# The level products of gated linear attention as 128-key matmuls, and as column tiles of 32 keys

## The chip, the core and the metric

The kernel runs on one core of a Trainium2 chip. The metric is the device time of one execution in microseconds, as the median of several runs: 2526.48 us before the change (three runs, 2525.47 to 2529.76). One more execution was taken with the hardware profiler; all rows come from it.

The engines appear in the profile as PE (matmuls) and PEld (the weight loads ahead of them), DVE (VectorE), ACT (ScalarE), POOL (GpSimd) and SP (the engine that issues most DMAs).

## The reference, cut to what matters

The model is one layer of a decoder trunk on a sequence of 2048 tokens with 1024 channels, in f32: a token mixer with three groups of heads (4 retention heads, 8 HGRN2 heads, 4 GLA heads), then a gated MLP with a short convolution. The change touches only the HGRN2 and GLA heads. Their recurrence, with a decay per key channel, is

```python
cum = jnp.cumsum(gn, axis=2)
rel = jnp.where(causal, cum[:, :, :, None, :] - cum[:, :, None, :, :], -jnp.inf)
attn = jnp.einsum('bhid,bhjd,bhijd->bhij', qn, kn, jnp.exp(rel))
o = jnp.einsum('bhij,bhje->bhie', attn, vn) + jnp.einsum('bhid,bhde->bhie', qn * jnp.exp(cum), s)
```

So query i meets key j with the product of all decays between them, channel by channel, and only for j up to i.

## The kernel before, in words

**Blocks and units.** The sequence is cut into 4 blocks of 512 tokens (TB), each into 4 chunks of 128 tokens. In a block the mixer works through seven units in the order h, g, h, h, h, r, r (ORDER, L35): four HGRN2 units of two heads (`unit_h`, L715), one GLA unit of four heads (`unit_g`, L754) and two retention units (`unit_r`, L799). Each unit first makes its projections: large matmuls on operands split into a high and a low part, three matmuls for one product (`split3`, L236). These are the bulk of PE's work. After the four blocks follow the out projection and the MLP.

**Levels.** A chunk's causal triangle is built by halving (`gated`, L618). For a level s of 1, 2, 4, ..., 64 (LEVELS, L604) tokens are grouped in blocks of 2s: the second half of each block are queries, the first half keys. `q` and `kq` already hold the decay up to the level's block borders, so one plain product gives the attention of all such pairs; then `q` and `kq` are multiplied by the decays of the next level (L648 and L650 on DVE) and the next level follows.

**The level product.** For each chunk L642 multiplies all 128 keys of the chunk with the 64 odd-half queries of each of two heads: 128 columns, written to 128 PSUM rows. Of each column only the s rows of the query's own block are wanted. A GLA unit has two parts of 64 channel rows each, whose products are issued in turn. A g unit so has 8 products for a level and an h unit 4. There are 16 h units and 4 g units, with 7 levels each: 112 h levels and 28 g levels.

**Taking out what is wanted.** For s up to 16 DVE copies all 512 columns from PSUM into the attention tile `at` (128 x 1024), under a mask `m_all` (L659, `copy_predicated`). For s of 32 and 64 ACT copies the wanted blocks (L656). `at` is set to zero before by POOL (L627). The attention tiles meet the values in `attn_out` (L600); the dot products of a token with itself are made apart (`dots`, L632).

**What sets the order.** PE's instructions stand in the order in which the program writes them. A planner (`Clock`, L55) interleaves the units' chains with the projections: each matmul moves a counter of microseconds on by an assumed price (`adv`, with M512 = 0.227 for a 512-column matmul and MF = 0.224 for an f32 product), and a chain's next step is due a gap later. After a level the gap is 3.2 us for h and 4.2 us for g (LEVEL_GAP, L51); projections fill it. A unit's chain begins when the one before has written its outputs' last step (`yield None`). The other engines' order is set by the scheduler from dependencies and priorities; what stands on an engine's queue waits in order, SP's and POOL's included. `lev` has two PSUM banks, `q` (`new_qbd`, L531, set to zero by POOL in L535) three buffers, `at` shares eight buffers of 4 KB. The table of rotary angles (`rope`, L802) has one buffer and is loaded once per block (L803) for the retention units. The masks are loaded by one DMA at the start (L1075); everything else of the first block is issued behind it.

**Other lines that the prediction uses.** L761 and L762 are a product with a weight of only 32 columns (`alow`, the low-rank gate of the GLA heads), which is written to PSUM rows 0 to 31. L664 are the transposes that follow a unit's last level. L597 are the products of queries with the state. L615 makes the decays of the levels. L820 is the first use of the rotary table.

Of the kernel before, what the change touches and what calls it, by code (L numbers as in the profile page):

```python
# [9 lines left out]
F32 = mybir.dt.float32  # L10
F32R = mybir.dt.float32r
I32 = mybir.dt.int32
U32 = mybir.dt.uint32
# [4 lines left out]
P = 128  # L18
# [28 lines left out]
HOT = 600  # L47
CHAIN = 400

M512, M256, MF = 0.227, 0.12, 0.224  # L50
LEVEL_GAP = (3.2, 4.2)  # L51
POST_GAP = 12.0

# [1 line left out]
class Clock:  # L55
# [15 lines left out]
    def adv(self, us):  # L71
        self.t += us
        while self.due and self.due[0][0] <= self.t:
            self._next()
# [26 lines left out]
def trunk(ctx, tc, xT, vecs, cvec, cst, rope, msk, wada, win, walow, wgla, wout, wup, wdown, out):  # L101
    nc = tc.nc
# [9 lines left out]
    pu = mix.enter_context(tc.tile_pool(name="unit", bufs=2))  # L112
    p1 = mix.enter_context(tc.tile_pool(name="const1", bufs=1))
    pp = ctx.enter_context(tc.tile_pool(name="ps", bufs=1, space=PSUM))
    clock = Clock()
    adv = clock.adv
# [4 lines left out]
    def lev_ps(name):  # L121
        return pp.tile([P, 512], F32, tag="lev", name=name, bufs=2)
# [3 lines left out]
    def late_ps(name):  # L126
        return pp.tile([P, 512], F32, tag="late", name=name, bufs=2)
# [10 lines left out]
    V, S, G, T = nc.vector, nc.scalar, nc.gpsimd, nc.tensor  # L138
# [1 line left out]
    vec = pc.tile([P, 117], F32, tag="vec", name="vec")  # L140
    nc.sync.dma_start(vec[:], vecs[:, 0:117])
    c_all = pc.tile([P, NC_], F32, tag="cst", name="c_all")
    m_all = p1.tile([P, 320], U32, tag="msk", name="m_all")
    ident = c_all[:, C_ID:C_ID + P]
    causal = c_all[:, C_CAUS:C_CAUS + P]
    ones = c_all[:, C_ONE:C_ONE + 1]
# [95 lines left out]
    h = [None] * KD  # L242
# [346 lines left out]
    def attn_out(name, b, attn, v, qn, Sst):  # L589


        ps = late_ps("o" + name)
        for c in range(NCH):
            oc = ps[:, c * P:(c + 1) * P]
            inter = not (b == 0 and c == 0)
            if inter:
                T.matmul(oc, qn[:, c * P:(c + 1) * P], Sst[:, (b * NCH + c) % NS, :], start=True, stop=False)  # L597
            for hh in range(2):
                at, col = attn[hh]
                T.matmul(oc[:, hh * 64:hh * 64 + 64], at[:, (c * 2 + col) * P:(c * 2 + col + 1) * P],  # L600
                         v[:, c, hh * 64:hh * 64 + 64], start=not inter, stop=hh == 1 or not inter)
        return ps
# [15 lines left out]
    def gated(name, b, ui, pos, kq, q, decay, subs, qk, sel):  # L618

        Sst = states[ui]  # L620
        tree, cur = decay
        two = len(subs) > 1
        parts = [slice(0, 64), slice(64, P)] if two else [slice(0, P)]
        attns = []
        for i, _ in enumerate(subs):
            at = pa.tile([P, 8 * P], F32, tag="a4k", name=f"at{name}_{i}")
            G.memset(at[:], 0.0)  # L627
            attns.append(at)
        nh = 2 * len(subs)
        ps = late_ps("dt" + name)  # L630
        for c in range(NCH):
            T.matmul(ps[:, c * nh:(c + 1) * nh], qk[:, c * P:(c + 1) * P], sel, start=True, stop=True)  # L632
        dots = pu.tile([P, NCH * nh], F32, tag="dots", name="dot" + name, bufs=3)
        S.copy(dots[:], ps[:, 0:NCH * nh])
        adv(4 * MF)
        for li, s in enumerate(LEVELS):
            nb = 64 // s
            pss = [lev_ps(f"lv{name}_{s}") for _ in parts]
            for c in range(NCH):
                for ps, rs in zip(pss, parts):  # L640
                    rhs = q[rs, :, c * P:(c + 1) * P].rearrange("p h (n t s) -> p h n t s", t=2, s=s)[:, :, :, 1, :]
                    T.matmul(ps[:, c * P:(c + 1) * P].rearrange("p (h n s) -> p h n s", h=2, s=s),  # L642
                             kq[rs, c * P:(c + 1) * P], rhs, start=True, stop=True)
            with tc.high_priority(offset=CHAIN):
                ev = tree[li]
                nn = TB // (2 * s)
                qv = q[:].rearrange("p h (n t s) -> p h n t s", t=2, s=s)[:, :, :, 1, :]
                V.tensor_tensor(qv, qv, ev[:, :, 0:1].unsqueeze(1).to_broadcast([P, 2, nn, s]), op=ALU.mult)  # L648
                kv = kq[:].rearrange("p (n t s) -> p n t s", t=2, s=s)[:, :, 0, :]
                V.tensor_tensor(kv, kv, ev[:, :, 1:2].to_broadcast([P, nn, s]), op=ALU.mult)  # L650
                for ps, at in zip(pss, attns):
                    dst = at[:].rearrange("p (a n t s) -> p a n t s", a=8, t=2, s=s)[:, :, :, 1, :]
                    src = ps[:].rearrange("p (a n s) -> p a n s", a=8, s=s)
                    if s >= 32:
                        for j0 in range(0, P, 2 * s):
                            S.copy(dst[j0:j0 + s, :, j0 // (2 * s), :], src[j0:j0 + s, :, j0 // (2 * s), :])  # L656
                    else:
                        mk = m_all[:, li * 64:li * 64 + 64].rearrange("p (n s) -> p n s", s=s)
                        V.copy_predicated(dst, mk.unsqueeze(1).to_broadcast([P, 8, nb, s]), src)  # L659
            adv(4 * MF)  # L660
            yield LEVEL_GAP[two]
        ps = late_ps("kT" + name)
        for c in range(NCH):
            T.transpose(ps[:, c * P:(c + 1) * P], kq[:, c * P:(c + 1) * P], ident)  # L664
        kT = pu.tile([P, NCH, P], F32, tag="kT", name="kT" + name, bufs=1)
        with tc.high_priority(offset=CHAIN):
            S.copy(kT[:].rearrange("p c n -> p (c n)"), ps[:])
            if not two:
                r0, r1 = subs[0][0][1]
                S.copy(q[r0:r1, 0, :], q[r0:r1, 1, :])  # L670
        adv(4 * MF)
        yield 1.8
        for rows, v, sg in subs:
            ps = late_ps("u" + name)
            for c in range(NCH):
                T.matmul(ps[:, c * P:(c + 1) * P], kT[:, c, :], v[:, c, :], start=True, stop=True)
            with tc.high_priority(offset=CHAIN):
                for c in range(NCH):
                    for hh, (r0, r1) in enumerate(rows):
                        es = slice(64 * hh, 64 * hh + 64)  # L680
                        dst = Sst[r0:r1, (b * NCH + c + 1) % NS, es]
                        u = ps[r0:r1, c * P + hh * 64:c * P + hh * 64 + 64]
                        if b == 0 and c == 0:
                            V.tensor_copy(dst, u)
                        elif c < NCH - 1 or b < NB - 1:
                            V.scalar_tensor_tensor(dst, Sst[r0:r1, (b * NCH + c) % NS, es], cur[r0:r1, c:c + 1], u,
                                                   op0=ALU.mult, op1=ALU.add)
        adv(4 * len(subs) * MF)
        yield 2.2
        os = []  # L690
        for i, (rows, v, sg) in enumerate(subs):
            if i:
                yield 2.2
            o = pu.tile([P, NCH, P], F32, tag="o", name=f"o{name}_{i}")
            dd = dots[:].rearrange("p (c h) -> p c h", h=nh)[:, :, 2 * i:2 * i + 2]
            o4 = o[:].rearrange("p c (h e) -> p c h e", e=64)
            with tc.high_priority(offset=CHAIN):
                V.tensor_tensor(o4, v[:].rearrange("p c (h e) -> p c h e", e=64),
                                dd.unsqueeze(3).to_broadcast([P, NCH, 2, 64]), op=ALU.mult)
            heads = [(at, i) for at in attns] if two else [(attns[0], hh) for hh in range(2)]  # L700
            ps = attn_out(f"{name}_{i}", b, heads, v, q[:, i, :], Sst)
            adv(12 * MF)
            with tc.high_priority(offset=CHAIN):
                V.tensor_tensor(o[:].rearrange("p c e -> p (c e)"), o[:].rearrange("p c e -> p (c e)"), ps[:],
                                op=ALU.add)
                post(o, sg, f"{name}_{i}")
            os.append(o)
        yield None
        for i, o in enumerate(os):
            yield POST_GAP if i == 0 else 3.0  # L710
            transposed(b, pos + i, o, f"{name}_{i}")
            adv(4 * MF)
# [356 lines left out]
    mk = {"h": unit_h, "g": lambda b, u, pos: unit_g(b, pos), "r": unit_r}  # L1069
    PE, DVE, ACT, SP = (getattr(mybir.EngineType, n) for n in ("PE", "DVE", "Activation", "SP"))  # L1070
    ctx.enter_context(tc.manual_schedule(engines={PE}))
    with tc.manual_schedule(engines={DVE, ACT, SP}):
        W0 = startup()
        last = gla_weights()
        first = [nc.sync.dma_start(m_all[:], msk[:, 0:320]).ins, *last]  # L1075
    jobs = [job for k in range(NF // 2) for job in (("d", k), ("u", 2 * k + 1 if k < 10 else 0))]
    behind = ExitStack()
    for ins in first:
# [538 lines left out]
```

## Time and profile before

| what | value |
|---|---|
| median of three runs | 2526.48 us |
| profiled execution, its own time | 2525.46 us |
| its span in the profile, first to last instruction | 2523.6 us |
| PE busy in the span | 2481.0 us, 98% |
| DVE busy | 1945.3 us, 77% |
| ACT busy | 1135.4 us, 45% |
| POOL busy | 159.7 us, 6% |
| mean granted TensorE clock | 0.996 |

The profile lists groups of instructions as line, engine, operation, output<-inputs with the tiles' names (lvh and lvg are the level banks of h and g units, ath and atg the attention tiles, X, Z, dX and others the MLP's banks), the shape, and the count. An f32 matmul appears as two records, each with its own weight load. A matmul's duration contains the way through the array, so successive matmuls overlap in the records; the distance of their starts tells what one costs. "128\*32" in a row means 128 contraction rows and 32 weight columns; "x512" the columns that stream through.

### The profile page before, as it was taken

The numbers are of one execution on the slowest core, as the hardware profiler recorded it, in microseconds if no ns is written. First come the engines' busy times: TensorE is split into PE (matmuls) and PEld (weight loads), VectorE is DVE, ScalarE is ACT, GpSimd is POOL, SyncE is SP. The second block draws the span as 40 slices with busy tenths as digits, with TensorE's granted clock in tenths as the row PEclk, the third lists the DMA queues.
The fourth block names the chain that finished last, engine by engine and source line by source line (L and its number), as shares of the span: only waits on it lengthen the run. The fifth ranks groups of instructions, "written<-read, shape, count | busy, mean of one in ns | idle before, by whom it ended". The sixth has DMA issues, their size and how long they took to land. (4 is left out here: it accounts for less than half of the span.)

```text
span 2523.6 us, 37047 instructions
## 1 busy us (share of the span) xinstructions
PE 2481.0 (98%) x13175; PEld 2110.3 (84%) x13175; DVE 1945.3 (77%) x3566; ACT 1135.4 (45%) x1913; POOL 159.7 (6%) x271
## 2 busy tenths in 40 slices
PE   7999999999999999999999999999999999999998
PEld 5888888888889888888888888888887888888887
DVE  7788976868678676767888888886688777778666
ACT  4443434423434235333455455455445554545542
POOL 1000000000000000000010000000001010010000
PEclk9999999999999999999999999999999999999999
DMA  8455576675687846885654544487665444447663
GB/s 296 174 190 171 207 266 210 230 270 200 220 325 260 284 156 235 289 295 177 235 184 148 170 149 141 159 299 240 209 222 180 153 138 153 152 132 259 222 194 124
DMA packets 228074, 524.95 MB, mean 208 GB/s; under 512 B 24968, under 2 KB 28080, under 8 KB 227888
## 3 DMA queue, kind: packets, MB, share of 16 engines
q1 hardware_dynamic: 224688, 512.08, 59.6%
q0 software_dynamic: 3200, 10.49, 1.2%
q8 instruction: 104, 1.70, 0.3%
q14 instruction: 82, 0.67, 0.1%
HBM read 392.97 MB, written 129.50 MB: 207 GB/s over the span
## 5 line engine op out<-in xcount | busy, mean ns | idle before, releaser
L238 PE MATMUL X<-B,A 128*128 128x512 f32 x572 | 223.1, 390 | 1.7 <-ACT u L1295 1.7
L239 PE MATMUL X<-B,A 128*128 128x512 f32 x572 | 222.6, 389 | 0.0
L240 PE MATMUL X<-B,A 128*128 128x512 f32 x572 | 222.5, 389 | 0.0
L1007 DVE TENSOR_TENSOR dA<-rd,dA 128x512 fp32r<-128x512 f32 x154 | 105.9, 689 | 90.4 <-ACT dA L1006 90.2
L1006 ACT CAST dA<-rd 128x512 fp32r<-128x512 f32 x154 | 95.5, 621 | 143.8 <-PE dX L240 57.3
L239 PE MATMUL dX<-dB,dA 128*128 128x512 f32 x396 | 154.2, 389 | 1.7 <-DVE dB L1007 1.7
L238 PE MATMUL dX<-dB,dA 128*128 128x512 f32 x396 | 154.1, 389 | 1.2 <-DVE y L1475 1.2
L240 PE MATMUL dX<-dB,dA 128*128 128x512 f32 x396 | 154.1, 389 | 0.0
L1007 DVE TENSOR_TENSOR A<-s,A 128x512 fp32r<-128x512 f32 x176 | 120.5, 685 | 38.6 <-ACT A L1006 38.5
L238 PE MATMUL psvgh<-hvgh,ha 128*128 128x256 f32 x480 | 140.8, 293 | 0.0
L1006 ACT CAST A<-s 128x512 fp32r<-128x512 f32 x176 | 108.6, 618 | 69.8 <-PE Z L240 40.3
L240 PE MATMUL psvgh<-hvgh,ha 128*128 128x256 f32 x480 | 136.4, 284 | 0.0
L239 PE MATMUL psvgh<-lvgh,ha 128*128 128x256 f32 x480 | 136.3, 284 | 0.0
L238 PEld LDWEIGHTS X<-B,A 128*128 128x128 f32 x572 | 107.4, 188 | 24.8 <-ACT u L1295 2.8
L240 PEld LDWEIGHTS X<-B,A 128*128 128x128 f32 x572 | 107.4, 188 | 22.4
L239 PEld LDWEIGHTS X<-B,A 128*128 128x128 f32 x572 | 107.4, 188 | 22.2
L239 PE MATMUL Z<-B,A 128*128 128x512 f32 x308 | 120.3, 390 | 1.6 <-DVE B L1007 1.6
L642 PE MATMUL lvh<-qbh,kh 128*128 128x128 f32 x896 | 120.2, 276 | 1.5 <-DVE nw L157 1.3
L642 PEld LDWEIGHTS lvh<-qbh,kh 128*128 128x128 f32 x896 | 114.7, 190 | 8.0 <-issue 2.0
L238 PE MATMUL Z<-B,A 128*128 128x512 f32 x308 | 120.3, 391 | 0.5 <-ACT B L1006 0.5
L240 PE MATMUL Z<-B,A 128*128 128x512 f32 x308 | 119.8, 389 | 0.0
L1007 DVE TENSOR_TENSOR A<-r,A 128x512 fp32r<-128x512 f32 x132 | 90.5, 686 | 26.4 <-ACT A L1006 26.1
(470 smaller groups left out, 7008.2 us busy)
## 6 DMA issues: line engine op xcount, KB each, us to landing
gs<-yv SPq DMA_DIRECT2D x154, 256.0 KB, 2.8
rb<-gs SPq DMA_DIRECT2D x154, 256.0 KB, 4.0
r<-wup SPq DMA_DIRECT2D x143, 256.0 KB, 3.3
s<-sumsu SPq DMA_DIRECT2D x132, 256.0 KB, 3.0
wada<-wada SPq DMA_DIRECT2D x48, 512.0 KB, 4.6
rd<-sumsd SPq DMA_DIRECT2D x88, 256.0 KB, 4.0
rd<-wdown SPq DMA_DIRECT2D x66, 256.0 KB, 3.8
x<-xT SPq DMA_DIRECT2D x64, 256.0 KB, 5.3
```

Source lines behind the costliest of these rows:

```text
L238: T.matmul(ps, lhs[0], rhs[0], start=first, stop=False, skip_group_check=more)
L239: T.matmul(ps, lhs[0], rhs[1], start=False, stop=False, skip_group_check=more)
L240: T.matmul(ps, lhs[1], rhs[0], start=False, stop=last, skip_group_check=more)
L642: T.matmul(ps[:, c * P:(c + 1) * P].rearrange("p (h n s) -> p h n s", h=2, s=s), kq[rs, c * P:(c + 1) * P], rhs, start=True, stop=True)
L1006: S.copy(hi, src)
L1007: V.tensor_tensor(lo, src, hi, op=ALU.subtract)
```

## The change

A level product is cut into pieces of w = max(32, 2s) tokens. For s up to 16 a chunk gives four products: 32 keys with the 32 odd-half queries (both heads) of the same 32 tokens, and each writes to the 32 PSUM rows of its keys, that is to its own strip of 32 columns of the PE array. For s = 32 there are two products of 32 keys with 64 columns, for s = 64 one of 64 keys with 128 columns. The four chunks lie side by side in the bank: a level of s up to 16 fills 128 columns instead of 512. An h unit has 16, 8 and 4 products for the three kinds of level, a g unit 32, 16 and 8.

For s up to 16 DVE copies these 128 columns under a smaller mask into a small tile `near` (128 x 8 x 32), which POOL sets to zero once per part of a unit. After level 16 ACT spreads `near` to its place in `at` with four copies of 32 rows and 256 columns. `near` has one buffer; the second one, of g units, shares the buffer of the rotary table (tag "rope"). The copies for s of 32 and 64 stay on ACT, with the same sizes. The masks are loaded by four DMAs of 32 rows. The planner counts 0.5 us (ML) for a level instead of 4 x MF = 0.896.

```diff
-M512, M256, MF = 0.227, 0.12, 0.224
+M512, M256, MF, ML = 0.227, 0.12, 0.224, 0.5
...
-    m_all = p1.tile([P, 320], U32, tag="msk", name="m_all")
+    m_all = p1.tile([P, 5, 16], U32, tag="msk", name="m_all")
...
-        attns = []
+        attns, nears = [], []
         for i, _ in enumerate(subs):
             at = pa.tile([P, 8 * P], F32, tag="a4k", name=f"at{name}_{i}")
             G.memset(at[:], 0.0)
             attns.append(at)
+            near = pu.tile([P, 8, 32], F32, tag="rope" if i else "near", name=f"near{name}_{i}", bufs=1)
+            G.memset(near[:], 0.0)
+            nears.append(near)
...
         for li, s in enumerate(LEVELS):
-            nb = 64 // s
+            w, keys = max(32, 2 * s), min(max(32, s), 64)
+            cols = slice(0, 8 * w // 2)
             pss = [lev_ps(f"lv{name}_{s}") for _ in parts]
             for c in range(NCH):
-                for ps, rs in zip(pss, parts):
-                    rhs = q[rs, :, c * P:(c + 1) * P].rearrange("p h (n t s) -> p h n t s", t=2, s=s)[:, :, :, 1, :]
-                    T.matmul(ps[:, c * P:(c + 1) * P].rearrange("p (h n s) -> p h n s", h=2, s=s),
-                             kq[rs, c * P:(c + 1) * P], rhs, start=True, stop=True)
+                for r0 in range(0, P, w):
+                    at = c * P + r0
+                    for ps, rs in zip(pss, parts):
+                        rhs = q[rs, :, at:at + w].rearrange("p h (n t s) -> p h n t s", t=2, s=s)[:, :, :, 1, :]
+                        T.matmul(ps[r0:r0 + keys, c * w:(c + 1) * w].rearrange("p (h n s) -> p h n s", h=2, s=s),
+                                 kq[rs, at:at + keys], rhs, start=True, stop=True)
...
-                for ps, at in zip(pss, attns):
-                    dst = at[:].rearrange("p (a n t s) -> p a n t s", a=8, t=2, s=s)[:, :, :, 1, :]
-                    src = ps[:].rearrange("p (a n s) -> p a n s", a=8, s=s)
-                    if s >= 32:
-                        for j0 in range(0, P, 2 * s):
-                            S.copy(dst[j0:j0 + s, :, j0 // (2 * s), :], src[j0:j0 + s, :, j0 // (2 * s), :])
+                for ps, at, near in zip(pss, attns, nears):
+                    if s <= 16:
+                        mk = m_all[:, li, :].rearrange("p (n s) -> p n s", s=s)
+                        V.copy_predicated(near[:].rearrange("p a (n t s) -> p a n t s", t=2, s=s)[:, :, :, 1, :],
+                                          mk.unsqueeze(1).to_broadcast([P, 8, 16 // s, s]),
+                                          ps[:, cols].rearrange("p (a n s) -> p a n s", a=8, s=s))
                     else:
-                        mk = m_all[:, li * 64:li * 64 + 64].rearrange("p (n s) -> p n s", s=s)
-                        V.copy_predicated(dst, mk.unsqueeze(1).to_broadcast([P, 8, nb, s]), src)
-            adv(4 * MF)
+                        for r0 in range(0, P, w):
+                            S.copy(at[r0:r0 + s, :].rearrange("p (a n) -> p a n", a=8)[:, :, r0 + s:r0 + 2 * s],
+                                   ps[r0:r0 + s, cols].rearrange("p (a n) -> p a n", a=8))
+                    if s == 16:
+                        for r0 in range(0, P, 32):
+                            S.copy(at[r0:r0 + 32, :].rearrange("p (a n) -> p a n", a=8)[:, :, r0:r0 + 32],
+                                   near[r0:r0 + 32])
+            adv(ML)
...
-        first = [nc.sync.dma_start(m_all[:], msk[:, 0:320]).ins, *last]
+        masks = msk[:, 0:320].rearrange("p (l n) -> p l n", n=64)
+        first = [nc.sync.dma_start(m_all[32 * g:32 * g + 32], masks[32 * g:32 * g + 32, :, 16 * g:16 * g + 16]).ins
+                 for g in range(4)] + last
```

## The prediction

> **What bounds the kernel now.** I read the table by stretches first, then the waits of PE, then the groups by line and shape, then the timeline around single levels.
>
> ```profile
> 63.00:350.00 287.00, 285.70 (x1824) 253.07 (x1824) 243.90 (x534) 116.02 (x215) 12.15 (x20) 1.00 0.56 196
> 960.00:1200.00 240.00, 237.85 (x1501) 207.69 (x1500) 169.64 (x402) 96.95 (x186) 13.72 (x22) 1.00 0.72 251
> 0.00:1200.00 1200.00, 1174.60 (x7308) 1027.50 (x7309) 915.81 (x2098) 478.66 (x886) 65.03 (x108) 1.00 0.67 235
> ```
>
> Columns: stretch, its length, then busy us (and count) of PE, PEld, DVE, ACT, POOL; PEclk, DMA share, GB/s. The mixer, where the change lies, is 0 to 1200 us. From 63 us on PE leaves 1.3 us of 287 and 2.2 of 240 free, at full clock. So what PE saves there shortens the run, and what another engine saves does not, unless PE waits for it. It hardly does:
>
> ```profile
> PE og L597 <- DVE S L686: 1.8, 1, 1.8
> PE psvgg L238 <- ACT qg L770: 1.4, 1, 1.4
> ```
>
> These two are the longest waits of PE between 60 and 1200 us (columns: us in all, times, longest). Now the level products, with the least, median and longest duration in ns; then a load of 32 columns; then groups by shape (busy us, mean ns):
>
> ```profile
> L642 PEld LDWEIGHTS lvh<-qbh,kh x896: 186/192/193, 63.3 to 1169.5; 128*128 128x128 f32 x180
> L642 PE MATMUL lvh<-qbh,kh x896: 270/275/362, 63.4 to 1169.6; 128*128 128x128 f32 x180
> L642 PEld LDWEIGHTS lvg<-qbg,kg x448: 182/188/188, 104.0 to 1041.0; 64*128 64x128 f32 x150
> L642 PE MATMUL lvg<-qbg,kg x448: 270/272/378, 104.0 to 1041.1; 64*128 64x128 f32 x150
> ```
> ```profile
> L761 PEld LDWEIGHTS alg<-ha,alow x32: 106/108/112, 53.4 to 973.1; 128*32 128x32 f32 x32
> ```
> ```profile
> L659 DVE COPY_PREDICATED ath<-m_all,lvh 128x512 f32<-128x512 uint32 x80 | 76.1, 951 | 0.0
> ...
> L659 DVE COPY_PREDICATED atg<-m_all,lvg 128x512 f32<-128x512 uint32 x40 | 36.9, 950 | 3.5 <-PE lvg L642 3.5
> ...
> L632 PE MATMUL dth<-c_all,qkh 128*128 128x2 f32 x128 | 15.9, 246 | 0.0
> ```
> ```profile
> L656 ACT COPY ath<-lvh 32x256 f32<-32x256 f32 x32 | 11.6, 363 | 51.8 <-PE lvh L642 50.2 <-issue 1.2
> ```
>
> Each f32 matmul is two passes here (448 products in 16 h units, 896 records), each pass a weight load and a matmul. A level of an h unit is 8 passes, of a g unit 16 (two halves of 64 rows). The durations contain the pipeline's latency, so what a level costs PE is read as delay in the timeline (start, duration):
>
> ```profile
> 67.35 0.39 PE L239 MATMUL psaqg<-ha,haqg 128*128 128x512 f32 x1
> 67.58 0.39 PE L240 MATMUL psaqg<-ha,laqg 128*128 128x512 f32 x1
> 67.81 1.07 PE L642 MATMUL lvh<-qbh,kh 128*128 128x128 f32 x8
> 68.63 0.48 PE L238 MATMUL psaqg<-ha,haqg 128*128 128x512 f32 x1
> 68.95 0.40 PE L239 MATMUL psaqg<-ha,haqg 128*128 128x512 f32 x1
> ```
> ```profile
> 109.81 0.39 PE L240 MATMUL pshfh<-ha,lhfh 128*128 128x512 f32 x1
> 110.12 1.18 PE L642 MATMUL lvg<-qbg,kg 64*128 64x128 f32 x16
> 111.23 0.50 PE L238 MATMUL pshqh<-ha,hhqh 128*128 128x512 f32 x1
> 111.57 0.39 PE L239 MATMUL pshqh<-ha,hhqh 128*128 128x512 f32 x1
> ```
>
> Projection matmuls start 0.23 us apart (67.35, 67.58). From 67.58 to 68.95 are 1.37 us for two steps (0.46) and the level: **0.91 us for an h level**. From 109.81 to 111.57: 1.76 less 0.46, **1.30 for a g level**. All: 112 x 0.91 + 28 x 1.30 = 138 us, the most the change can touch.
>
> **The change part by part.** *One pass.* A weight load of 128 columns takes 190 ns (188 to 192), of 32 columns 108: 82 ns for 96 columns, so 27 ns for 32 and 109 for 128. That this load sets the pace shows in dth: 8 passes of only 2 columns are 15.9/16 = 0.99 us busy, less the last's 0.246, over 7 steps 0.107 each. A level pass is 0.91/8 = 0.114, stream and load side by side. So a pass of 32 keys by 32 columns is 27 ns of load beside at most 27 of stream: 0.032 us with the same 5 ns on top.
>
> *Do four column tiles run side by side?* No row shows it. The nearest: the g level does 16 passes in little more time than an h level does 8, so two row tiles do run together; its 1.30 is 8 x 0.114 = 0.91 plus 0.39 for going in and out. For column tiles the only row is the product of alow, 32 weight columns wide:
>
> ```profile
> 358.35 0.39 PE L240 MATMUL y<-oTr,lwo 128*128 128x512 f32 x1
> 358.58 0.39 PE L761 MATMUL alg<-ha,alow 128*32 128x512 f32 x1
> ...
> 360.20 0.40 PE L762 MATMUL alg<-ha,alow 128*32 128x512 f32 x1
> 360.44 0.38 PE L597 MATMUL oh<-S,qbh 128*128 128x128 f32 x2
> ```
>
> In 0.23, out 0.24: the plain step, no toll. [...]
>
> *Levels 1 to 16.* The 8 passes of a part and level become 4 chunks x 4 tiles x 2 passes = 32. Bounds: with the four tiles fully side by side each has 8 passes, 8 x 0.032 + 0.03 for the first load = 0.28; one after the other 32 x 0.032 = 1.02. Between them lies a third case: the two passes of a product follow each other on their tile, and only the next product runs beside them, 16 x 0.032 = 0.51. I take **0.45**, just below that, because the g row, the nearest, shows tiles that overlap almost fully. No toll is added, by the alow row. For g there are 64 passes on eight tiles: 0.28 + 0.39 = 0.67 at least, 1.02 + 0.39 = 1.41 at most. I take **0.80**, nearer to the lower end for the same reason.
>
> *Level 32.* Two tiles of 64 columns, 55 ns of stream: 8 x 0.06 + 0.03 = **0.51** (up to 16 x 0.06 = 0.96); g 0.51 + 0.39 = **0.90**. *Level 64.* One tile of 64 keys and 128 columns, stream as before: **0.91** and **1.30**.
>
> Sum: h unit 7 x 0.91 = 6.37 before, 5 x 0.45 + 0.51 + 0.91 = 3.67 after, -2.70 x 16 = -43.2. g unit 9.10 before, 5 x 0.80 + 0.90 + 1.30 = 6.20, -2.90 x 4 = -11.6. **PE: -54.8 us**, ends -71 and +12.
>
> *DVE.* The 120 masked copies fall from 512 elements to 128.
>
> ```profile
> L648 DVE TENSOR_TENSOR qbh<-qbh,eh 128x512 f32<-128x512 f32 x96 | 65.9, 686 | 38.8 <-PE lvh L642 38.0
> ...
> L615 DVE TENSOR_TENSOR eh<-eh 128x128 f32<-128x128 f32 x16 | 4.6, 289 | 0.3
> ```
>
> A plain product of two tiles goes from 0.69 to 0.29 us between these sizes; the masked copy takes 0.95/0.69 = 1.4 times the plain one, so 0.40 after: 120 x 0.55 = 66 us less on DVE. It is off the path: the next level's products wait for L648 and L650, which stand ahead of the copy, and PE's waits on DVE in the mixer are a few us in all. Value 0, between -5 (those waits gone) and 0.
>
> *ACT.* New: four copies of 32x256 per part at level 16, 24 parts, 96 x about 0.38 (L656's 0.363 from PSUM) = 36 us. They wait for the masked copy on DVE; behind them on ACT stand level 32's copies, weight casts and evacuations, for which PE waits. Cover: ACT is 40% busy (478.66 of 1200), and L656 already sits 50 us in front of lvh without a PE wait on the list. Value **+4**, between 0 and +36 if nothing covered them.
>
> *POOL.* 24 memsets of near (256 columns) join those of the attention tiles (L627), on an engine busy 65 of 1200 us. near has one buffer, so its memset waits until the unit before has spread it at level 16. Behind it on POOL stand the q memsets (L535), which wait for the output products (L597) of an earlier unit, and the first masked copy of the next unit waits for near itself:
>
> ```profile
> 102.98 1.09 POOL L535 MEMSET qbh<- 64x512 f32 x2 [57.93 <-PE oh L597]
> ```
>
> POOL stood still for 57.93 us in front of this one anyway, and the output products come two levels after the spread. So near's wait is over first: 0. If that cover went, the masked copies of the new unit's level 1 would be late, and with them the level banks.
>
> *SP.* near's second tile takes the place of the rope table:
>
> ```profile
> L820 DVE TENSOR_TENSOR rb0r<-ra0r,roper x8: 417/422/426, 233.6 to 1172.9; 128x256 f32<-128x256 f32 x8
> ...
> L803 SPq DMA_DIRECT2D roper<-rope x4: 328/376/509, 55.2 to 877.9; - x4
> ```
> ```profile
> L664 PE MATMUL kTg<-c_all,kg x16: 270/272/273, 147.1 to 1046.0; 128*128 128x128 f32 x16
> ```
> ```profile
> L1075 SPq DMA_DIRECT2D m_all<-msk x1: 420/420/420, 40.2 to 40.2; - x1
> ```
>
> The first rope load cannot go at 55.2 any more, but after g's level 16, which is over before g's transposes at 147; it is needed at 233.6. Moved down SP's queue it costs 0; left in its place, every load queued behind it would stand for up to 90 us. Three more mask loads are 3 x 0.42 = 1.3 us of SP at 40 us; behind them is the key projection's weight load (L225), in front of a PE that there waits for its first inputs: 0 to +1, value 0.
>
> *Order of the work.* The planner now counts 0.5 for a level instead of 0.896. The gaps that it fills with projections (3.2 and 4.2 us) stay, so between two levels stand as many projections as before, and a unit's chain only ends 7 x 0.4 = 2.8 planner's us earlier: 0.
>
> Sum: -54.8 + 4 = -50.8. The profiled execution took 2525.5 (span 2523.6 and 1.9 around it): 2474.7; the median shown is 1.0 higher: **2476 us**.
>
> **The rivals.**
> *1. The h levels pay g's toll of 0.39 too.* Levels 1 to 16 at 0.28 + 0.39 = 0.67, level 32 at 0.90, level 64 at 1.30: 5.55 per unit, -0.82 x 16 = -13; g as forecast: 2526.5 - 13 - 11.6 + 4 = 2506. For: the g rows. Against: the alow rows.
>
> *2. The four tiles share one path for weights or columns.* h unit 5 x 1.02 + 0.96 + 0.91 = 6.97, +0.60 x 16 = +9.6; g 5 x 1.41 + 1.35 + 1.30 = 9.70, +0.60 x 4 = +2.4; with ACT's 4: 2543. For: load time goes by columns (108 against 190 ns), and the sum of columns loaded is unchanged. Against: g's two row tiles load and stream together.
>
> *3. PE's sequencer does not deliver the instructions fast enough (the slower side).* Between two levels of an h unit stand 3.2 us of projections, 14 passes or 28 instructions; with the 64 of a level they are 92, in 3.65 us: 40 ns each. In g 4.2 us hold 37, with 128 of a level 165, in 5.0 us: 30 ns.
>
> ```profile
> 418.93:425.21 6.28, 6.28 (x65) 6.02 (x66) 5.35 (x9) 1.30 (x3) 0.00 (x0) 1.00 0.73 252
> ```
>
> The densest stretch of that length now has 131 in 6.28 us, 48 ns each, so 40 is shown nowhere. At x ns per instruction levels 1 to 16 of all units (80 of h, 20 of g, 4.11 and 5.50 us with their gaps now) change by 80 x (0.092x - 4.11) + 20 x (0.165x - 5.50), and level 32 gives 8 back: the sign turns at **42 ns**. At 48 it is +65, with ACT's 4 **2596**. For: 40 is asked of every level, and nowhere shown. Against: in g's level 32 instructions pass in about 1.1 us, 34 ns each, though only 32.
> *4. Small passes have a fixed price of their own*, whatever their size, and start x ns apart. [...] The rows leave x open: g's 16 passes in 0.91 us are 57 ns each, dictated by their weight loads. [...]
>
> *5. Half the gain is lost to waits on ACT and DVE*: Closer levels ask for copies and evacuations sooner, and DVE is 85% busy in the first block (243.90 of 287); against it, DVE gets 66 us less to do. 2526.5 - 25 = 2501.
>
> **How the numbers follow.** Forecast (2452 to 2500) 0.49, rival 1 0.12, rival 5 0.05: faster, 0.66. Rival 4 0.05: within 0.2% (about what a measurement of this kernel can tell from no change). Rival 2 0.12, rival 3 0.17: slower, 0.29. From -71 us with nothing lost (2455) to rival 2 with half of ACT's copies uncovered (2556) lies 0.82; rival 3 is left out. Range 2452 to 2556.
>
> **What would show it.** Right: 2944 h passes and 1472 g passes on the level line; from the projection matmul ahead of a level to the second one behind it about 0.91 us (0.46 + 0.45) in h for levels 1 to 16; masked copies of 128 elements near 0.40 us; no wait of PE on ACT's copies beyond the 1.4 us seen. Rival 1: same toll at level 64. Rival 2: about 1.0 per level. Rival 3: projection matmuls behind a level spread to more than 0.23 apart, PE idle with "issue". Wrong above all would be a level above 0.9, or PE waiting for ACT's spread or for near's memset.

## The result, and the profile after

The changed kernel takes 2489.76 us (median of four runs, 2488.3 to 2490.3), against 2527.95 us (2525.47 to 2529.76) for the kernel before, measured beside it: a ratio of 0.9849 with a 95% interval of 0.9832 to 0.9866, 38 us less. The profiled execution took 2489.37 us, its span is 2487.6, so 36.0 less than the 2523.6 of before.

All of it is won in the mixer: the last output product (L600 in both kernels) starts at 1174.2 us instead of 1210.5, 36.3 earlier. First the stretches, with the columns of the prediction's first fence; the mixer now ends at 1175.

```profile
63.00:350.00 287.00, 284.42 (x2769) 240.57 (x2769) 230.28 (x545) 131.32 (x249) 14.42 (x27) 1.00 0.61 206
960.00:1175.00 215.00, 214.81 (x2065) 184.31 (x2064) 146.34 (x380) 92.28 (x188) 10.95 (x20) 1.00 0.79 274
```

PE is as full as before (2.6 and 0.2 us free), with more and smaller instructions. So the gain is the PE time that the levels gave up, and nothing else was let in. The longest waits of PE between 60 and 1200 us are still single ones, and no row names ACT's spread or `near`'s memset:

```profile
PE lvh L648 <- DVE kh L656: 4.0, 1, 4.0
PE pshfh L239 <- DVE ha L350: 1.1, 1, 1.1
```

The groups of the three lines that the change made (L648 is the level product, L660 the masked copy, L669 the spread; least, median and longest ns):

```profile
L648 PE MATMUL lvh<-qbh,kh x2944: 189/196/323, 63.4 to 1134.1; 128*32 128x32 f32 x171, 128*32 128x64 f32 x17, 128*64 128x128 f32 x9
L648 PE MATMUL lvg<-qbg,kg x1472: 186/193/320, 102.5 to 1009.6; 64*32 64x32 f32 x160, 64*32 64x64 f32 x16, 64*64 64x128 f32 x8
...
L660 DVE COPY_PREDICATED nearh<-m_all,lvh x80: 284/296/455, 65.1 to 1126.5; 128x128 f32<-128x128 uint32 x80
...
L669 ACT COPY ath<-nearh x64: 387/405/412, 82.2 to 1128.2; 32x256 f32<-32x256 f32 x64
```

The counts are the forecast ones: 2944 and 1472 passes, 120 masked copies, 96 spread copies. The masked copy takes 0.30 us (forecast 0.40), the spread copy 0.40 (0.38).

What a level costs PE is read as in the prediction: from the start of the last projection matmul before it to that of the second one behind it, less two steps of 0.23. The timeline of the changed kernel around an h level of the first five, h's level 64, a g level, and the product of `alow` (start, duration):

```profile
79.74 0.39 PE L240 MATMUL psvgg<-hvgg,ha 128*128 128x512 f32 x1
80.06 0.46 PE L648 MATMUL lvh<-qbh,kh 128*32 128x32 f32 x32
80.45 0.50 PE L238 MATMUL psvgg<-hvgg,ha 128*128 128x512 f32 x1
80.79 0.39 PE L239 MATMUL psvgg<-lvgg,ha 128*128 128x512 f32 x1
...
87.95 0.39 PE L240 MATMUL psvgg<-hvgg,ha 128*128 128x512 f32 x1
88.27 1.09 PE L648 MATMUL lvh<-qbh,kh 128*64 128x128 f32 x8
89.29 0.50 PE L238 MATMUL psvgg<-hvgg,ha 128*128 128x512 f32 x1
89.63 0.40 PE L239 MATMUL psvgg<-lvgg,ha 128*128 128x512 f32 x1
...
107.86 0.39 PE L240 MATMUL pshfh<-ha,lhfh 128*128 128x512 f32 x1
108.17 0.76 PE L648 MATMUL lvg<-qbg,kg 64*32 64x32 f32 x64
108.86 0.50 PE L238 MATMUL pshqh<-ha,hhqh 128*128 128x512 f32 x1
109.19 0.40 PE L239 MATMUL pshqh<-ha,hhqh 128*128 128x512 f32 x1
...
349.45 0.40 PE L240 MATMUL y<-oTr,lwo 128*128 128x512 f32 x1
349.68 0.40 PE L772 MATMUL alg<-ha,alow 128*32 128x512 f32 x1
...
350.38 0.39 PE L773 MATMUL alg<-ha,alow 128*32 128x512 f32 x1
350.61 0.38 PE L597 MATMUL oh<-S,qbh 128*128 128x128 f32 x2
350.83 0.33 PE L600 MATMUL oh<-vh,ath 128*128 128x64 f32 x2
```

Look at the first level. Its 32 passes are in the records for 0.46 us; less the 0.20 of the last one, the last pass starts 0.26 after the first. Four tiles with eight passes each in 0.26 us are 33 ns a pass: the tiles run fully side by side. But the level begins 0.32 behind the projection matmul (79.74 to 80.06), where a plain level begins 0.23 behind it (67.58 to 67.81 in the kernel before), and the second projection matmul is 0.34 behind the first (80.45 to 80.79) instead of 0.23. That is the toll which the forecast left out. In three parts: 0.09 going in (0.32 less 0.23), 0.09 coming out (the first projection matmul is 0.12 behind the last pass, where the next pass would be 0.03 behind), and 0.11 at the step after it. The last part is seen in the weight loads of the changed kernel, here behind the g level:

```profile
108.86 0.19 PEld L238 LDWEIGHTS pshqh<-ha,hhqh 128*128 128x128 f32 x1
```

The load starts with its own matmul (108.86 both), not 0.22 ahead of it as between plain matmuls (the next load starts at 108.97, its matmul at 109.19), and PE stands for it. The step behind a plain level is as long in the records (68.63 to 68.95 in the prediction's timeline of an h level), but there the load starts at 68.60, together with the last pass of the level, and runs beside that pass, so nothing is lost.

The medians of these delays over the levels that have projections on both sides, and the sum that they give for all 140 (microseconds):

| levels | number | before | after | forecast | PE, all levels |
|---|---|---|---|---|---|
| h, 1 to 16 | 80 | 0.890 | 0.582 | 0.45 | -24.6 |
| h, 32 | 16 | 0.890 | 0.766 | 0.51 | -2.0 |
| h, 64 | 16 | 0.890 | 1.212 | 0.91 | +5.2 |
| g, 1 to 16 | 20 | 1.288 | 0.879 | 0.80 | -8.2 |
| g, 32 | 4 | 1.288 | 0.78 | 0.90 | -2.0 |
| g, 64 | 4 | 1.288 | 1.22 | 1.30 | -0.3 |

Together -31.9 us. (For g's levels 32 and 64 the matmuls around them have partly 256 columns; the steps taken off are then 0.12 and 0.23.) The rest stands inside the levels of before. Five g levels were held up in the middle, waiting for a level bank that a masked copy (0.95 us in the mean) was still reading:

```profile
116.22 0.49 PE L642 MATMUL lvg<-qbg,kg 64*128 64x128 f32 x2
117.04 1.13 PE L642 MATMUL lvg<-qbg,kg 64*128 64x128 f32 x14 [0.33 <-DVE atg L659]
```

This is the timeline of the kernel before: the two rows are one g level of 1.95 us (117.04 + 1.13 - 116.22) where an undisturbed one has 1.18. In 21 h levels of before, mostly the first level of a unit, which stands right behind the short products of `dots`, the second pass starts 0.20 behind the first instead of 0.11. No wait is recorded there; the weight load of the first pass starts less than 0.05 ahead of it, in the other 91 h levels 0.12 to 0.23. Over all levels, what the way from first to last pass exceeds the median of its kind adds up to 4.8 us before (2.7 in g, of the first sort, and 2.1 in h, of the second) and 0.2 after. -31.9 and -4.6 make -36.5; the span gives -36.0.

### The profile page after: what moved, and what is told of

The parts are those of the page before. It is cut to its first block, busy times and chain, and to the rows that moved or that the text cites. A ratio compares the mean times of both kernels' runs of the same rounds, so it can differ in the third digit from the quotient of the medians.

```text
span 2487.6 us, 43325 instructions
## 1 busy us (share of the span) xinstructions
PE 2443.5 (98%) x16247; PEld 2044.6 (82%) x16247; DVE 1877.2 (75%) x3566; ACT 1175.3 (47%) x2009; POOL 167.9 (7%) x295
## 5 line engine op out<-in xcount | busy, mean ns | idle before, releaser
L1018 DVE TENSOR_TENSOR A<-s,A 128x512 fp32r<-128x512 f32 x176 | 120.8, 687 | 36.3 <-ACT A L1017 36.2
L1017 ACT CAST A<-r 128x512 fp32r<-128x512 f32 x132 | 82.3, 623 | 65.5 <-PE Z L240 58.3
L1018 DVE TENSOR_TENSOR dB<-rb,dB 128x512 fp32r<-128x512 f32 x154 | 105.6, 688 | 9.0 <-ACT dB L1017 8.8
```

Source lines behind the costliest of these rows:

```text
L1017: S.copy(hi, src)
L1018: V.tensor_tensor(lo, src, hi, op=ALU.subtract)
```

## The experiments

The theory, **A**: a level product that uses less than the full array costs its passes side by side and on top a fixed toll of about 0.29 us for going in and coming out, and the product of `alow` pays none because its operands are f32r, not f32. The rivals were that small passes cost more by themselves, that a tile position other than the first is what costs, and that DVE, ACT or the planner took the missing gain. Ratios are to the kernel before on the same chip; the changed kernel has 0.9849.

**Twice the passes, the same toll** (the level products of levels 1 to 16 are issued twice into the same bank).

```diff
-            for c in range(NCH):
+            for c in list(range(NCH)) * (2 if s <= 16 else 1):
```

> The products of levels 1 to 16 are issued twice (same values, the planner's price unchanged), so that a level has 64 passes in an h unit and 128 in a g unit. Theory A (four tiles run side by side, and what a level costs beyond its stream is a fixed toll for entering and leaving the tiled mode): only the stream doubles, 0.26 us more in each of 80 h levels (first to last pass start now 0.263) and 0.56 in each of 20 g levels: +32 us against the changed kernel, about 2522. Theory B (the cost is per pass, no toll): each h level costs 0.58 more and each g level 0.88 more: +64 us, about 2554. Theory C (PE's sequencer is near its limit at 40 ns per instruction): 64 more instructions per interval, over 100 us more.

Measured: 2539.19 us, ratio 1.0049 (1.0033 to 1.0064). Its timeline around an h level and a row of PE's waits that the changed kernel doesn't have:

```profile
80.77 0.39 PE L240 MATMUL psvgg<-hvgg,ha 128*128 128x512 f32 x1
81.09 0.76 PE L648 MATMUL lvh<-qbh,kh 128*32 128x32 f32 x64
81.78 0.50 PE L238 MATMUL psvgg<-hvgg,ha 128*128 128x512 f32 x1
82.12 0.39 PE L239 MATMUL psvgg<-lvgg,ha 128*128 128x512 f32 x1
```
```profile
PE lvg L648 <- issue: 3.0, 2, 1.8
```

The level grows from 0.46 to 0.76 in the records, so 0.30 for 32 more passes, while the way in (0.32) and the second step behind (0.34) stay. All h levels: 0.886 instead of 0.582, +0.304. Were it the passes that cost the missing 0.3, the level would have doubled. In the whole time the run lies midway between theories A and B; what decides is the single level. In g it is +0.53. The levels then explain 80 x 0.304 + 20 x 0.53 = 35 us; the span is 47 longer. Of the other 12, PE's idle time in the mixer (21.4 us against 10.7) explains most, and 6.6 us of it are new waits with "issue", in which PE waited for nothing that the profile shows. In g the doubling cost 8.3 ns a pass (0.53 us for 64), though eight tiles stand ready there, twice h's four; the next experiment shows where the time goes.

**One more way out and in** (in the middle of each level 1 to 16 a plain product of 128 x 128 weights and 2 columns, into an unused part of the bank).

```diff
+                if c == 2 and s <= 16:
+                    T.matmul(pss[0][:, 256:258], ident, selh, start=True, stop=True)
```

> In levels 1 to 16 one plain product (128 rows, 128 weight columns, 2 columns streamed, into unused columns of the level bank) is put between the second and the third chunk, so that each level leaves and enters the tiled mode once more. Theory A (a toll per entry and exit): two passes of about 0.11 and a toll of about 0.3 more per level, 100 levels: +45 to +55 us against the changed kernel, about 2540. Theory B (no toll, only passes): two passes of 0.11, +22 us, about 2512.

Measured: 2526.72 us, ratio 0.9988 (0.9978 to 0.9997), some 35 us above the changed kernel, between the figures of the theories.

```profile
81.56 0.39 PE L240 MATMUL psvgg<-hvgg,ha 128*128 128x512 f32 x1
81.88 0.33 PE L650 MATMUL lvh<-qbh,kh 128*32 128x32 f32 x16
82.14 0.38 PE L645 MATMUL lvh<-c_all 128*128 128x2 f32 x2
82.45 0.33 PE L650 MATMUL lvh<-qbh,kh 128*32 128x32 f32 x16
82.72 0.50 PE L238 MATMUL psvgg<-hvgg,ha 128*128 128x512 f32 x1
83.05 0.40 PE L239 MATMUL psvgg<-lvgg,ha 128*128 128x512 f32 x1
```

An h level now takes 1.030, +0.448. Two plain passes alone are 0.22 (the 0.107 a step of the product dth in the prediction, twice), so a way out and in cost 0.23. That is less than 0.29: the plain product pays the first two parts of the toll (82.14 to 82.45 is 0.31 for two passes of 0.11, and 0.12 lie before it) and the third is already counted: the load of its first pass isn't fetched ahead either (at the g level of this version load and pass both start at 110.94), but it is one of the two loads of 0.11 that make up the 0.22. The last 0.05 are not assigned.

A g level takes only 0.20 more, for the same way out and in. Its rows in this version:

```profile
110.66 0.35 PE L650 MATMUL lvg<-qbg,kg 64*32 64x32 f32 x32
110.94 0.38 PE L645 MATMUL lvg<-c_all 128*128 128x2 f32 x2
111.26 0.35 PE L650 MATMUL lvg<-qbg,kg 64*32 64x32 f32 x32
111.54 0.50 PE L238 MATMUL pshqh<-ha,hhqh 128*128 128x512 f32 x1
```

Each half of 32 passes takes 0.35 in the records; less the 0.19 of one pass, its last pass starts 0.16 after its first: 5 ns a pass. The undivided level of the changed kernel takes 0.76 less 0.19, 0.57 for 64 passes. So two halves need 0.16 each, and in one piece 0.57: in the single records the 33rd pass starts 0.07 us behind the 32nd, and soon after the passes come two by two, 17 ns apart. The 64 passes of a doubled h level start within 0.56 us (0.76 less 0.20), 9 ns apart in the mean. With their loads the late passes of g come at about 4 ns an instruction (17 ns for two passes and two loads). It may be rival 3 in a mild form; no run tests that, nor what ends the fast part. Whatever the reason, it costs g 0.24 a level, 20 x 0.24 = 4.7 us. The levels give 80 x 0.448 + 20 x 0.20 = 40 us more; PE's idle time in the mixer is 2.5 shorter (8.2 against 10.7), and the span is 37.9 longer.

**What spares `alow` its toll** (its operands read as f32 instead of f32r; shape and place in the array stay).

```diff
-            T.matmul(ps[0:32, :], alow[:, k, :], h[k][:, 0, :], start=(k == 0), stop=False)
-            T.matmul(ps[0:32, :], alow[:, k, :], h[k][:, 1, :], start=False, stop=(k == KD - 1))
+            T.matmul(ps[0:32, :], alow[:, k, :].bitcast(F32), h[k][:, 0, :].bitcast(F32), start=(k == 0), stop=False)
+            T.matmul(ps[0:32, :], alow[:, k, :].bitcast(F32), h[k][:, 1, :].bitcast(F32), start=False, stop=(k == KD - 1))
```

> The 32-column product of alow, which in the trace before entered and left at the plain step of 0.23 us, is made in f32 instead of the f32r type (same position, PSUM rows 0 to 31, twice the passes). If the f32r type is what spares it the toll, its first pass now starts about 0.3 us after the projection matmul ahead of it, and the matmul behind it is late too. If single-position tiles are free whatever the type, the step stays at 0.23. In time the passes add 4 x 16 x 0.2 to 0.9 us, 15 to 55 us, which is not the question.

Measured once: 2533.34 us, 43.6 above the changed kernel's median. The timeline at the same place as the last rows of the changed kernel above:

```profile
358.93 0.40 PE L240 MATMUL y<-oTr,lwo 128*128 128x512 f32 x1
359.25 1.05 PE L772 MATMUL alg<-ha,alow 128*32 128x512 f32 x2
360.13 1.02 PE L773 MATMUL alg<-ha,alow 128*32 128x512 f32 x2
...
361.85 1.02 PE L773 MATMUL alg<-ha,alow 128*32 128x512 f32 x2
362.80 0.49 PE L597 MATMUL oh<-S,qbh 128*128 128x128 f32 x2
363.13 0.33 PE L600 MATMUL oh<-vh,ath 128*128 128x64 f32 x2
```

Going in takes 0.32 instead of 0.23. From the last pair to L597 are 0.95 instead of the pair's own 0.86. L597's two passes take 0.33 instead of 0.22. The same three parts as at a level, 0.09, 0.09 and 0.11, at the first position of the array and with 512 columns. So for this product the type decides (with the second pass that comes with it), not the position and not the size: the narrow product pays in f32 and doesn't in f32r. Full 128 x 128 products in f32 don't pay either, as the h levels of before show (0.23 in, 67.58 to 67.81). Count and type can be read in the rows: `x1` for one L772 matmul here above, `x2` in f32. (The 40 us of its time are the passes: 64 matmuls at 2 x 0.43 instead of 0.23.)

**The toll at level 64, where it buys nothing** (h's level 64 multiplies all 128 keys again, as before; only the wanted rows are copied).

```diff
             w, keys = max(32, 2 * s), min(max(32, s), 64)
+            keys = P if s == 64 and not two else keys
```

> In h units level 64 is multiplied with all 128 keys again, as before the change, so that it needs no tiled mode; its wanted 64 rows and their copy stay. Theory A (toll of about 0.3 us per tiled level, and nothing won in stream there): the level falls from 1.21 to about 0.90 us, 16 x 0.32 = 5 us faster than the changed kernel, about 2484.5. If the toll were not the level's own, no change.

Measured: 2484.37 us (2481.98 to 2486.45), ratio 0.9835 (0.9817 to 0.9853).

```profile
88.36 0.39 PE L240 MATMUL psvgg<-hvgg,ha 128*128 128x512 f32 x1
88.58 1.05 PE L649 MATMUL lvh<-qbh,kh 128*128 128x128 f32 x8
89.39 0.48 PE L238 MATMUL psvgg<-hvgg,ha 128*128 128x512 f32 x1
89.71 0.40 PE L239 MATMUL psvgg<-lvgg,ha 128*128 128x512 f32 x1
```

The same eight passes with the same 128 columns, and 0.89 instead of 1.21: half the keys cost more than all. 16 x 0.32 = 5.2 us forecast, 3.5 by the ratios. Since that was small and on another chip, both were run again side by side:

> The changed kernel itself, once more, so that it stands beside the next kernel on one chip: ratio to the kernel before 0.985 as at first (0.983 to 0.987).

> The version whose h level 64 keeps all 128 keys, beside the changed kernel on one chip. Theory A (the toll at level 64 buys nothing: 16 times 0.32 us): 5 us less than the changed kernel, ratio to the kernel before about 0.983. Theory B (the first comparison, on two chips, was chance): no difference.

The changed kernel 2490.30 us, 0.9847 (0.9834 to 0.9861); with the full level 64 2488.51 us, 0.9836 (0.9822 to 0.9850). Twice the ratio is lower by 0.0011 to 0.0014, some 3 us, but the intervals overlap. That each level 64 is 0.32 cheaper is shown; the gain in the whole time is likely, not settled. Its two ratios are the lowest of all versions.

**DVE's share** (each masked copy three times, 55 us more DVE work).

```diff
-                        V.copy_predicated(near[:]...
+                        for _ in range(3):
+                            V.copy_predicated(near[:]...
```

> Each masked copy into near is made three times (same result): 240 more copies of 128 columns, about +95 us on DVE, which gives DVE back more than the change took from it (68 us). Theory A (the gain is PE's alone, DVE is off the path): the time stays within 5 us of the changed kernel's 2489.8. Rival (DVE's relief carries part of the gain): 15 us or more slower.

Measured: 2495.58 us, ratio 0.9867 (0.9853 to 0.9882), about 4.5 us more. The 240 copies more take 0.30 us each in the records, 72 us together, but DVE's busy time rises by only 55 (1932.4 against 1877.2). That is less than was counted on, and less than the 68 us that the change took off DVE, so the run doesn't give back all of it. Of the 55 about a twelfth reaches the end: DVE is nearly off the path. The waits for the level banks do not come back either. The three copies of a level take 0.9 us again, as the one copy did before, and yet g's levels are held for 0.2 us in all and not for 2.7. So it isn't shown that the shorter copy alone did away with those waits.

**ACT's share** (the spread issued twice: 96 copies of 0.40, 39 us more on ACT).

```diff
-                        for r0 in range(0, P, 32):
+                        for r0 in [*range(0, P, 32)] * 2:
```

> Each of the four spreading copies of near into the attention tile is made twice: 96 more copies on ACT, about +40 us of ACT. The prediction put +4 us on the first 96. Theory A (ACT covers them): within 2 us of the changed kernel's 2489.8. Rival (they cost what was put on them or more): +4 us or more.

Measured: 2499.65 us, ratio 0.9882 (0.9865 to 0.9899), about 8 us more. The first row of PE's waits:

```profile
PE lvg L648 <- ACT atg L665: 4.3, 6, 2.2
```

The level bank of g is held by level 32's copies, which stand behind the spread on ACT. In the first profile of the changed kernel this row is missing; in a second profile of it (with the runs of 2490.30 us) it stands with one wait of 0.3 us. So the first 39 us just fit under the cover, and the next don't.

**The spread on POOL** (in the version with the full level 64).

```diff
-                            S.copy(at[r0:r0 + 32, :]...
+                            G.tensor_copy(at[r0:r0 + 32, :]...
```

> The version whose h level 64 keeps its full width (2484), with the 96 spread copies issued on POOL instead of ACT: 38.8 us of ACT (96 x 0.404) go. Theory A (in the changed kernel the spread is covered: PE's list of waits has no row for it, and only its doubling cost 8 us): no gain, 2481 to 2487, and g's level 64 keeps its delay of 1.22. Theory B (the forecast's +4: part of it is paid somewhere off PE's list): 2 to 6 us less, 2478 to 2482. Theory C (POOL is slower per copy than ACT and the output products then wait for the attention tile): 2490 or more, with a wait of PE on a POOL copy of the spread line.

Measured: 2491.29 us, ratio 0.9854 (0.9840 to 0.9867), some 5 us more than the 0.9835 and 0.9836 of that version, with overlapping intervals, and no wait of PE on a POOL copy. Theory B's gain did not come, the time lies above the range of A, and C's mechanism is not in the list. PE's idle time in the mixer is 17.0 us, against 10.4 and 12.7 in the two profiles of that version; the longer waits are on DVE, among them one of 2.2 us of the transposes (L676, for DVE's L657) that was not there. Why DVE is later with the spread on POOL is open. What follows: taking the 39 us off ACT brought no gain here.

**The planner's price.** First alone in the kernel before, 0.5 for a level instead of 0.896:

```diff
-            adv(4 * MF)
+            adv(0.5)
```

> The kernel before the change, with only the planner's price of a level set to 0.5 instead of 0.896. The prediction put this at 0: within 3 us of 2527. If closer chains matter, it moves by more.

Measured: 2533.16 us, ratio 1.0029 (1.0017 to 1.0041), 7 us slower, with longer waits of PE on DVE; the first row is one that the kernel before doesn't have:

```profile
PE dth L632 <- DVE oh L704: 4.4, 2, 2.5
```

Then the old price in the changed kernel, and in the one with the full level 64:

```diff
-            adv(ML)
+            adv(4 * MF)
```

> The changed kernel with only the planner's price of a level put back from 0.5 to 0.896 of its microseconds. Measured on PE a level now costs 0.58 (levels 1 to 16 of h), 0.77, 1.21 and in g 0.88, 0.78, 1.22, 0.74 in the mean of the 140: 0.5 is 0.24 too low, 0.896 is 0.16 too high. In the kernel before, whose mean is 0.97, the step from 0.896 to 0.5 alone cost 7 us. Theory A (a price too low lets the planner believe that more fits between two levels than does, a price too high costs little): 2 to 5 us less than the changed kernel, 2485 to 2488. Theory B (what counts is the distance from the truth on either side): within 2 us of the changed kernel. Theory C (the lower price is right for the faster levels and its undoing costs what it cost before): 4 to 7 us more.

> The same price on top of the version whose h level 64 keeps its full width (that one was 4 to 5 us faster than the changed kernel). Theory A: another 2 to 5 us off, 2479 to 2483 us; theory B: within 2 us of 2484; theory C: 4 to 7 us more, 2488 to 2491.

Measured: 2492.09 us, 0.9857 (0.9839 to 0.9876), and 2492.03 us, 0.9859 (0.9837 to 0.9881). Against 0.9849 and 0.9835 that is 2 and 6 us slower, with overlapping intervals. Theory A, a gain, falls; between B and C it is not settled. The price of 0.5 costs 7 us where levels take 0.97 in the mean; where they take 0.74 no cost of it can be seen.

## Why the prediction was right and where it was wrong

The forecast was 2476 us in a range of 2452 to 2556, faster with 0.66. It came out faster, at 2489.8, 14 us above the likeliest value: of 51 us forecast 36 came.

- **What bounds.** Right: PE. 55 us of DVE work more cost some 4 us, 39 of ACT some 8, and 35 us of PE work more in the levels cost 47 to 50.
- **One pass, and four tiles side by side.** Right: 33 ns against 32. With it rival 2 falls (about 1.0 per level). But the forecast didn't go by it: full overlap gave 0.28 by its own working, and it took 0.45, between that and two passes in turn. Without the toll a level's passes take 0.29 (0.582 less 0.29). So 0.16 of the missing toll was covered by a reserve that had been put there for something else. That is luck: with 0.28 and no toll the h levels 1 to 16 would have missed by 80 x 0.30 = 24 us and not by 10.6.
- **"No toll is added, by the alow row".** This is the step that failed. Each narrow level pays about 0.29 us, and of h's forecast of -43.2 us -21.4 came. The three terms are 0.13 more for each level 1 to 16 (80 x 0.13 = 10.6), 0.26 at level 32 (4.1) and 0.30 at level 64 (4.8; the forecast started from 0.91). The mechanism was rival 1's, which was given 0.12 and put the toll at g's 0.39. At 0.29 it is cheaper, and the rows of before show why: in a g level the second pass on a tile starts 0.22 behind the first, the others 0.11. So 0.11 of the 0.39 is the first load of 128 columns, which isn't fetched ahead either (load and pass both start at 110.12); a first load of 32 columns adds 0.02 (in the h levels of the changed kernel the second pass on a tile starts 0.05 behind the first, the third 0.03 behind the second). The error lay in the row, not in the arithmetic: the product of `alow` was taken as the nearest because its shape was the same, and its type was not looked at. The prediction itself says that an f32 product shows as two records. `alow`'s row had x32, one for each of the 8 x 4 matmuls of its line. It was another kind of product. The g rows, in f32, were the nearer ones, and they said toll. The trace of before has one more such row, which the prediction passed over: the product that follows `alow`'s, with `gup` (L772 of the kernel before, 32 rows, f32, two records), between projections:

```profile
70.57 0.40 PE L240 MATMUL psaqg<-ha,laqg 128*128 128x512 f32 x1
70.90 1.12 PE L772 MATMUL zg<-alg,gup 32*128 32x512 f32 x2
71.95 0.50 PE L238 MATMUL psvgg<-hvgg,ha 128*128 128x512 f32 x1
72.28 0.40 PE L239 MATMUL psvgg<-lvgg,ha 128*128 128x512 f32 x1
```

Going in takes 0.33 instead of 0.23, the two passes of 0.43 and the way out 1.05 instead of 0.86, the step behind 0.33 instead of 0.23: together 0.39, as in g. Like `alow`'s product it is narrow and streams 512 columns, and yet it pays; that would have raised the question of the type.

- **Levels 32 and 64.** Level 32 of h saves 0.12 instead of 0.40. Level 64, "unchanged", got slower by 0.32 (rival 1 had 0.39): going narrow there halves the keys, and the passes stay eight.
- **g.** Nearly right: -10.5 us against -11.6. Its toll was there before and stays. 0.88 for 0.80, of which 0.24 is the slow second half of the burst; levels 32 and 64 a little cheaper than forecast.
- **DVE.** 68 us less (1877.2 against 1945.3) for 66. The copy came down to 0.30 and not 0.40, because 0.95 was a mean of copies of 0.69 to 1.36 us; their median, 0.72, is little above the plain product's 0.69. Value 0, "between -5 and 0": PE's waits for the banks inside g's levels went, 2.7 us, within that range. Their cause is not isolated (see DVE's share).
- **ACT.** Busy +40 (1175.3) for +36; of the value +4 nothing is seen in PE's waits but 0.3 us, once, in one of two profiles, for level 32's copies behind the spread. But doubling it costs 8, so the cover was nearly used up.
- **POOL and SP.** 0, right: neither has a row in PE's waits.
- **Order of the work.** Value 0 fits the changed kernel, but its reason ("the gaps stay") doesn't: alone in the kernel before the same price costs 7 us.
- **Rivals 3 and 4.** Not as they were priced: an h level's 64 instructions go out in 0.26 us, 4 ns each, where rival 3 turned at 42. The price of a pass at which rival 4 would have meant no change is shown by no run; the passes of an h level start 8 ns apart, the first 32 of a g level 5. Something of rival 3's kind shows at 17 ns for two passes beyond the first 32, and only g's levels lose by it.
- **Rival 5.** Not so: PE's idle time in the mixer is 10.7 us, 10.8 before.

Left open: what ends the fast part of a burst after 32 passes, why `alow`'s product pays no toll in f32r, what removed the waits inside g's levels, why DVE is late with the spread on POOL, and whether the planner's price matters in the changed kernel.

## What to carry to other kernels

Before a row is taken as the nearest, compare its type and its count of records with the operation to come, not its shape alone. In f32, a stretch of products on part of the array between plain matmuls pays 0.29 us here, whether it has 8 passes or 64, and 0.39 where its weights have 128 columns. Make a product narrow only where that saves more (level 1: 0.6 saved; level 64: nothing), and put many narrow products into one stretch, here best up to 32 passes (the second 32 of a g level lose 0.24 us). When single steps are compared by their medians, add up also what some steps lose inside, by waits or by a load that comes late; here that was 4.6 us of 36.

## What the runs showed of the hardware

- Four column tiles of 32 with f32 weights, all on the same 128 rows, load and multiply fully side by side in the h levels of the changed kernel: 32 passes start within 0.26 us, 8 ns apart, though one load of 32 columns is in the records for 0.11 us.
- In g's levels 1 to 16, with eight tiles, the first 32 passes start 5 ns apart; the 33rd starts 0.07 to 0.08 us behind them, and soon after come two passes every 17 ns, 8.4 ns a pass. All 20 of these levels show it.
- The toll of `alow`'s product, with 32 weight columns, came with its type: none in f32r (0.23 in and out, the only such product here), and in f32 the three parts of together 0.29 us (0.09, 0.09 and 0.11) that the narrow levels pay too. On top comes what the first weight load, which isn't fetched ahead, adds: 0.11 for 128 columns (g's levels before), 0.02 for 32 (h's levels after).
- A pass of 512 columns in f32 takes 0.43 us (two from 360.13 to 360.99, in the version with `alow` in f32), and such a product is in the records as two; in f32r it is one of 0.23.
